# Attention in a diffusion trunk: 128-row low-part score products and a TensorE order written by hand

## The chip, the cores and the metric

One core of one Trainium2 chip runs the whole program in one launch. The metric is device time in microseconds (us); smaller is better. Five engines work side by side, each through its own queue in order: PE (TensorE: matrix products and transposes), DVE (VectorE), ACT (ScalarE), POOL (GpSimd) and SP (which issues the transfers). PEld is the loading of the stationary operand, which runs beside PE.

## The reference

The model has four layers over 256 context tokens and 256 latent tokens of 1024 features, all in float32. The third layer mixes the tokens by grouped-query attention: 16 query heads and 4 key heads of 64 features, so four query heads share a key head. Context queries see the 256 context keys, latent queries see all 512. Queries and keys are normed per head, and those of latent tokens are rotated (`rope`).

```python
def sdpa(q, k, v):
    s = jnp.einsum('bkgqd,bksd->bkgqs', q, k).astype(jnp.float32) * ATTN_SCALE
    p = jax.nn.softmax(s, axis=-1).astype(v.dtype)
    return jnp.einsum('bkgqs,bksd->bkgqd', p, v)
...
        q, k, v = jnp.split(z, [ATTN_Q_DIM, ATTN_Q_DIM + ATTN_KV_DIM], axis=-1)
        q = rms_norm(q.reshape(B, L, ATTN_KV_HEADS, ATTN_GROUP, ATTN_HEAD_DIM), g_q).transpose(0, 2, 3, 1, 4)
        k = rms_norm(k.reshape(B, L, ATTN_KV_HEADS, ATTN_HEAD_DIM), g_k).transpose(0, 2, 1, 3)
...
        if rope:
            q = apply_rope(q, cos, sin)
            k = apply_rope(k, cos, sin)
...
    y_ctx = merge(sdpa(qc, kc, vc))
    k_all = jnp.concatenate([kc, kl], axis=2)
    ob = lax.map(lambda qq: sdpa(qq, k_all, v_all), qb)
```

The other layers (two of gated linear attention, one of convolution), the squared-ReLU MLP behind each, and the modulation are not touched by the change.

## The kernel before

Activations and weights are split exactly into a high part (12 bits, written as float32r) and a low part, and a product is made of three: high with high, low with high, high with low. Tokens stand in four tiles of 128: t=0 and 1 are context, t=2 and 3 latent.

The attention layer (`attn`) projects keys and values first (`prep_kv`), then the queries of eight heads; the other eight heads' queries (`q_steps`) are projected in chunks of six products that `plan` spreads among the first steps of the score loop. `turned` transposes blocks of queries or keys on PE into PSUM, and `evac` copies them out: on ACT, but each EV-th (EV = 100) on DVE.

Queries are kept as 128 rows: 64 rows of the high part and 64 of the low part of the same head (`q2`; in the other order for odd key heads). The keys' high part stands twice, one copy under the other (`k2`), so one product over 128 rows gives high with high and low with high. The keys' low parts of two key heads lie one under the other in one tile (`kl`), and the third product reads the 64 rows of its head alone:

```python
r = slice(64 * (kv % 2), 64 * (kv % 2) + 64)
mm(out=sc[b][:, 0:nk * P], lhsT=q[r], rhs=kl[kv // 2][r, 0:nk * P], start=False, stop=True)
```

The score loop has 32 steps: eight pairs of heads (`hp`), and for each the token tiles in the order t = 2, 3, 0, 1. A step's scores (line 1197 with `k2`, line 1199 with `kl`, for both heads) have 512 columns for latent and 256 for context queries; softmax follows (maximum on DVE, exponential with its sum on ACT, reciprocal and scaling on DVE). `values` then transposes the probabilities (`pTp`, line 1220, 128 x 128 each: eight in a latent step, four in a context step), copies them out (`pT`), and multiplies with the values (`o`, line 1226, of which each fills 64 of the 128 output rows; again eight or four). The loop calls `values` LAG = 3 steps behind the scores:

```python
pend.append((hp, t, o, scores(hp, t)))
if len(pend) > LAG:
    second(*pend.pop(0))
```

This sets priorities only. A scheduler at build time puts each engine's instructions into their final order. In it one `o` product is often followed by transposes, the other `o` products and more transposes, and the scores of one step are split around them. The two heads' `o` products of a chunk stand next to each other in the source, and write the upper and the lower 64 rows of the output.

PSUM has two banks for transposes, four for scores (the fourth from step 12 on), and two that take turns for `o`. `st` tiles come from a pool of 45.

Of the kernel before, what the change touches and what calls it, by code (L numbers as in the profile page):

```python
# [14 lines left out]
P = 128  # L15
# [14 lines left out]
# columns of the packed per-feature parameters  # L30
# [34 lines left out]
LAG = 3  # L65
EV = 100
# [11 lines left out]
def kernel(ctx: ExitStack, tc: tile.TileContext, io, out, depth=8):  # L78
# [19 lines left out]
    def load_table(name):  # L98
        """Loads a table once for the functions traced from here on: behind those traced before."""
        load = nc.scalar.preload_act_table_set(name)  # L100
        for user in table["users"]:
            behind(load.ins, user)
        table.update(name=name, load=load.ins.name, users=[])
# [67 lines left out]
    # work that may run whenever the tensor engine would wait: the next layers' modulation  # L171
# [49 lines left out]
    def project(srcs, acts, streams, done, first=3, extra=0, tail=0, apart=False, then=None):  # L221
        """Feature-major products of the units in srcs with acts. The first few run side by side, so
        that they start with the first activations; apart, the streams of the first few and of the
        last few run one after the other, next to the other stream's norm."""
# [30 lines left out]
    def project_tm(srcs, acts, parts, done, between=lambda z: None, order=(0, 1, 2, 3), before=None):  # L255
        """Token-major products [token, 512] of four units of two k each; parts are lists of token
        tiles that run one after the other."""
# [36 lines left out]
    def mod_sum(i, b, n, kk, got):  # L294
        """The same on VectorE, for the time when the tensor engine is full: both streams' sums over
        the feature tiles, whose partitions the tensor engine adds up at the end."""
# [72 lines left out]
    def spread(cols, blocks, tag="nr"):  # L369
        """[token, block] columns to rows, the same on all partitions."""  # L370
        ps = bank("rows", tag)
        for n, b in enumerate(blocks):
            mm(out=ps[:, b * P:b * P + P], lhsT=cols[:, n:n + 1].to_broadcast([P, P]), rhs=ident,
               start=True, stop=True)
        return ps

    def sums(srcs, blocks):
        """Sums over features (the partitions of all srcs) to [token, block]."""
# [9 lines left out]
    def square(k, zs):  # L388
        """Adds the squares of x's feature tile k, as soon as it is final, to the sums for the norm."""
# [30 lines left out]
    def normed(n, z, rs=None):  # L420
        """The norm of stream z ahead of sub-layer n."""
# [9 lines left out]
    def out_project(n, srcs, acts, streams, gate, bias=None, **kw):  # L431
        """The last product of sub-layer n, added to x, and the next sub-layer's norm."""
# [52 lines left out]
    def gla(i, j, last, first=None):  # L485
# [6 lines left out]
        # low-rank gates, four copies of the rank rows  # L492
# [14 lines left out]
        def start_with(kk):  # L507
            """The norm of two feature tiles as soon as their modulation is there."""
# [7 lines left out]
        # values, token-major  # L516
# [15 lines left out]
        # cumulative log gates  # L532
# [48 lines left out]
        def r_unit(m):  # L581
            def done(ps):
                # the Silu with the functions of the gates' table: r exp(-ln(1 + exp(-r)))
# [11 lines left out]
        def weave(*threads):  # L595
            """Emits threads of steps side by side, the first thread's step first."""
# [5 lines left out]
        def blocks(tl, c, lo=0):  # L602
            """The chunks c of each block from lo on."""
            return tl.rearrange("p (b c t) -> p b c t", c=2, t=CH)[:, lo:, c]

        def prep(hh):
            """Decayed queries and keys and the states of a head, a thread per direction. Tiles of
            which a direction needs only one chunk per block hold both directions."""
            shared = {}

            def direction(d):
# [10 lines left out]
                def products():  # L622
# [11 lines left out]
                    # queries: with the decay since the chunk's start, then since the block's  # L634
# [4 lines left out]
                def ends():  # L639
                    kb, ebv, kd, kx, e = got["kb"], got["ebv"], shared["kd"], b, got["e"]  # L640
                    # keys: with the decay to the chunk's end, then to the block's
# [19 lines left out]
                def carry():  # L661
                    # states ahead of each block, in the direction's order
# [19 lines left out]
        def core(hh):  # L682
            op, at = [], {}

            def inner(bl):
# [12 lines left out]
                # within a chunk: forward up to the query, backward from it on, both at it  # L698
# [71 lines left out]
        # the rank rows in two parts of 12 bits, so that one product with the weights' parts holds  # L770
        # all four products of the parts
# [23 lines left out]
    def conv(i):  # L795
# [29 lines left out]
        def on_dve(c, zs):  # L825
            """The steps of a feature tile's depthwise convolution on VectorE."""
# [21 lines left out]
        def split(c, zs):  # L848
            """Both parts of u of each stream, with zeros around it."""
# [11 lines left out]
        def on_pe(c, zs):  # L861
            """The same on the tensor engine, with diagonal matrices."""
# [26 lines left out]
        # [tile, tap, high or low part], the middle tap first  # L889
# [12 lines left out]
        def merge(old, new):  # L902
            """Puts the steps of new between those of old: the taps of a tile wait for one another."""
# [30 lines left out]
        def layer_norm(z):  # L934
            """The steps of the LayerNorm over features and the Silu."""
# [47 lines left out]
            def staged(*stages):  # L983
                """One step per tile; each stage a tile, or as many as its lag, behind the one before."""
# [12 lines left out]
        def norm_with(z, *queues):  # L997
            """The LayerNorm, with steps of other work between its steps."""
# [21 lines left out]
    def attn(i):  # L1020
# [7 lines left out]
        # [position, q or k, lat tile, feature]: gain times cos, and the signed gain times sin for  # L1028
        # the half-swapped operand
# [345 lines left out]
```

## Time and profile before

| what | value |
|---|---|
| time, median of 3 runs | 2244.36 us (2243.71 to 2244.63) |
| span of the profiled execution | 2243.1 us |
| PE busy | 2194.2 us, 98% |
| DVE busy | 1627.2 us, 73% |
| ACT busy | 871.5 us, 39% |
| PE in the chain that ended last | 90% of the span |
| granted PE clock, mean | 0.990 |

The profiled execution is shown by its span, from its first to its last instruction; the median of the timed runs is 1.3 us above it, which is what lies around the instructions. A PE record begins when the product begins and its end is modelled, so neighbouring products overlap in the records: the price of a product is read from the start of one to the start of the next.

### The profile page before, as it was taken

To read this page: it belongs to the slowest core of one execution; us is meant where nothing else is said; L and a number is where in the kernel's file an instruction comes from. 1 tells how busy PE (TensorE), PEld (TensorE's weight loads), DVE (VectorE), ACT (ScalarE), POOL (GpSimd) and SP (SyncE) were. 2 spreads that over 40 slices of the span, in tenths; PEclk is the share of its full clock that TensorE was granted. 3 is DMA by queue.
4 is the path that set the end of the run, shared out by engine and by line. 5 is a ranking of instruction groups with operands and counts; after the bars stand their busy time and mean duration, and the time that the engine had idled before them with its cause. 6 is when DMAs were issued, how large, how long until landed. Compare 5 with 4: busy or idle time off the path is not lost.

```text
span 2243.1 us, 33453 instructions
## 1 busy us (share of the span) xinstructions
PE 2194.2 (98%) x13154; PEld 1858.6 (83%) x13154; DVE 1627.2 (73%) x2968; ACT 871.5 (39%) x1504; POOL 56.6 (3%) x68
## 2 busy tenths in 40 slices
PE   6999999999999979999999999999999999999999
PEld 5777898888888979988888876688888889899999
DVE  4565577788869986768888677647788776687665
ACT  4443343223232205532232367634232324555443
POOL 0000000000000251000000000000000000000000
PEclk9999999999999979999999999999999999999999
DMA  8543334555522111345555211014465552233553
GB/s 302 170 150 132 116 101 153 177 178 195 198 95 82 33 38 39 105 156 171 179 189 195 85 50 54 20 48 150 142 196 182 194 169 77 93 113 127 186 182 119
DMA packets 83966, 299.58 MB, mean 134 GB/s; under 512 B 9440, under 2 KB 10976, under 8 KB 83808
## 3 DMA queue, kind: packets, MB, share of 16 engines
q1 hardware_dynamic: 83808, 297.44, 40.0%
q8 instruction: 104, 1.70, 0.3%
q14 instruction: 54, 0.44, 0.1%
HBM read 296.35 MB, written 1.05 MB: 133 GB/s over the span
## 4 chain that ended last, share of the span: by engine, by line
PE 90%; DVE 7%; ACT 1%; issue 1%; POOL 0%; DMA 0%; SPq 0%; DVEq 0%; POOLq 0%
PE ps L217 21%; PE ps L218 21%; PE ps L219 21%; DVE cv L841 4%; PE one L217 2%; PE one L218 2%; PE one L219 2%; PE ps L274 2%; PE ps L276 2%; PE ps L275 2%; PE o L1226 2%; PE pTp L1220 1%; PE cvps L881 1%; PE o L718 1%; PE modps L291 1%; PE sc L1199 1%
## 5 line engine op out<-in xcount | busy, mean ns | idle before, releaser
L109 ACT ACTIVATE whi<-raw 128x1024 fp32r<-128x1024 f32 x366 | 387.1, 1059 | 887.3 <-PE ps L218 621.5
L196 DVE TENSOR_TENSOR wlo<-raw,whi 128x1024 fp32r<-128x1024 f32 x366 | 445.1, 1225 | 164.3 <-ACT whi L109 163.3
L217 PE MATMUL ps<-hi,whi 128*128 128x512 f32 (+1 forms) x1336 | 464.1, 348 | 0.0
L219 PE MATMUL ps<-hi,wlo 128*128 128x512 f32 (+1 forms) x1336 | 461.5, 346 | 0.0
L218 PE MATMUL ps<-lo,whi 128*128 128x512 f32 (+1 forms) x1336 | 461.3, 345 | 0.0
L217 PE MATMUL ps<-hhi,whi 128*128 128x512 f32 (+1 forms) x1240 | 437.8, 355 | 3.3 <-ACT hhi L109 3.3
L218 PE MATMUL ps<-hlo,whi 128*128 128x512 f32 (+1 forms) x1240 | 438.4, 354 | 0.0
L219 PE MATMUL ps<-hhi,wlo 128*128 128x512 f32 (+1 forms) x1240 | 436.8, 353 | 0.0
L307 DVE SCALAR_TENSOR_TENSOR macc<-modraw,cs,macc 128x512 f32<-128x512 f32 x504 | 346.8, 744 | 0.0
L217 PEld LDWEIGHTS ps<-hi,whi 128*128 128x128 f32 x1336 | 252.9, 189 | 33.9 <-issue 3.7
L219 PEld LDWEIGHTS ps<-hi,wlo 128*128 128x128 f32 x1336 | 253.1, 189 | 30.7 <-issue 0.2
L218 PEld LDWEIGHTS ps<-lo,whi 128*128 128x128 f32 x1336 | 253.2, 190 | 29.8
L217 PEld LDWEIGHTS ps<-hhi,whi 128*128 128x128 f32 x1240 | 234.4, 190 | 38.4 <-ACT hhi L109 4.0
L219 PEld LDWEIGHTS ps<-hhi,wlo 128*128 128x128 f32 x1240 | 235.2, 190 | 31.6
L218 PEld LDWEIGHTS ps<-hlo,whi 128*128 128x128 f32 x1240 | 235.5, 190 | 30.9
L448 DVE SCALAR_TENSOR_TENSOR x<-ps,mod,x 128x256 f32<-128x256 f32 x264 | 118.6, 480 | 173.6 <-PE ps L219 172.1
L841 DVE SCALAR_TENSOR_TENSOR cv<-u,par,cv 128x498 f32<-128x498 f32 (+28 forms) x210 | 129.4, 679 | 0.4
L109 ACT ACTIVATE hi<-sq 128x512 fp32r<-128x512 f32 (+1 forms) x128 | 73.8, 576 | 104.4 <-DVE sq L463 104.4
L217 PE MATMUL one<-hhi,whi 128*128 128x512 f32 (+1 forms) x256 | 95.2, 372 | 0.3 <-DVE r L588 0.3
L203 DVE TENSOR_TENSOR lo<-sq,hi 128x512 fp32r<-128x512 f32 (+1 forms) x128 | 79.3, 620 | 22.1 <-ACT hi L109 22.1
L218 PE MATMUL one<-hlo,whi 128*128 128x512 f32 (+1 forms) x256 | 91.6, 358 | 0.0
L219 PE MATMUL one<-hhi,wlo 128*128 128x512 f32 (+1 forms) x256 | 91.1, 356 | 0.0
(213 smaller groups left out, 2792.4 us busy)
## 6 DMA issues: line engine op xcount, KB each, us to landing
modraw<-in_w_mod SPq DMA_DIRECT2D x192, 512.0 KB, 3.7
raw<-in_w_mlp_in SPq DMA_DIRECT2D x128, 512.0 KB, 4.1
raw<-in_w_mlp_out SPq DMA_DIRECT2D x128, 512.0 KB, 3.5
raw<-in_conv_pw SPq DMA_DIRECT2D x24, 512.0 KB, 3.4
raw<-in_gla_v SPq DMA_DIRECT2D x16, 512.0 KB, 3.7
raw<-in_gla_r SPq DMA_DIRECT2D x16, 512.0 KB, 3.8
raw<-in_gla_out SPq DMA_DIRECT2D x16, 512.0 KB, 3.9
raw<-in_attn_qkv SPq DMA_DIRECT2D x12, 512.0 KB, 3.4
```

The costliest lines, as they stand in the source:

```text
L109: ins = nc.scalar.activation(**kw).ins
L196: tt(out=lo, in0=raw, in1=hi.bitcast(F32), op=ALU.subtract)
L203: tt(out=lo[:, cols], in0=src, in1=hi.bitcast(F32)[:, cols], op=ALU.subtract)
L217: mm(out=o, lhsT=wh[:, wsl], rhs=ah[:, cols], start=first, stop=False)
L218: mm(out=o, lhsT=wh[:, wsl], rhs=al[:, cols], start=False, stop=False)
L219: mm(out=o, lhsT=wl[:, wsl], rhs=ah[:, cols], start=False, stop=last)
L274: mm(out=ps[t], lhsT=ah[:, tok], rhs=wh[:, sl], start=kk == order[0] and i == 0, stop=False)
L275: mm(out=ps[t], lhsT=al[:, tok], rhs=wh[:, sl], start=False, stop=False)
L276: mm(out=ps[t], lhsT=ah[:, tok], rhs=wl[:, sl], start=False, stop=kk == order[-1] and i == 1)
L307: stt(out=acc, in0=raw[:, h], scalar=c, in1=acc, op0=ALU.mult, op1=ALU.add)
L448: stt(out=x[:, m, c], in0=src[:, c], scalar=gate[:, m, z:z + 1], in1=x[:, m, c], op0=ALU.mult, op1=ALU.add)
L841: ins = stt(out=a3[:, :, lo:hi], in0=u3[:, :, lo + s:hi + s], scalar=tap, in1=a3[:, :, lo:hi], op0=ALU.mult, op1=ALU.add).ins
```

## The change

There are two parts. First, the low parts of the keys are doubled as the high parts already are: `klo` holds each head's 64 features twice (one more ACT copy in each of four token tiles), `turned` makes four transposes of it instead of two, there are four `kl` tiles instead of two, and the low-part product contracts all 128 rows. It then also adds low with low.

Second, `values` is cut into `turned_p` (transposes and copies) and `values` (products). The score loop is put in a `manual_schedule` for PE, so that PE's order is the source's: in step n the scores of n, the value products of n-3, the transposes of n-2 (LAG_T = 2, LAG_O = 1). The other engines are still ordered by the scheduler. Besides, EV goes from 100 to 5, so that each fifth copy out of PSUM is made by DVE.

```diff
-LAG = 3
-EV = 100
+LAG_T = 2
+LAG_O = 1
+EV = 5
...
-        q2, k2, kl = {}, [st("k2", FR) for _ in range(4)], [st("kl", FR) for _ in range(2)]
+        q2, k2, kl = {}, [st("k2", FR) for _ in range(4)], [st("kl", FR) for _ in range(4)]
...
-                tt(out=lo.rearrange("p (h e) -> p h e", e=64), in0=got["q"], in1=h4.bitcast(F32)[:, :, 0],
-                   op=ALU.subtract)
+                tt(out=l4[:, :, 0], in0=got["q"], in1=h4.bitcast(F32)[:, :, 0], op=ALU.subtract)
+                act(out=l4[:, :, 1], in_=l4.bitcast(F32)[:, :, 0], func=ACTF.Copy)
...
-                r = slice(64 * (kv % 2), 64 * (kv % 2) + 64)
-                mm(out=sc[b][:, 0:nk * P], lhsT=q[r], rhs=kl[kv // 2][r, 0:nk * P], start=False, stop=True)
+                mm(out=sc[b][:, 0:nk * P], lhsT=q, rhs=kl[kv][:, 0:nk * P], start=False, stop=True)
...
+        def turn_scores():
+            hp, t, o, ps = scored.pop(0)
+            turned_.append((hp, t, o, turned_p(ps, t)))
+
+        def add_values():
+            hp, t, o, pts = turned_.pop(0)
+            values(pts, hp, t, o)
...
-                pend.append((hp, t, o, scores(hp, t)))
-                if len(pend) > LAG:
-                    second(*pend.pop(0))
+        with tc.manual_schedule(engines={mybir.EngineType.PE}):
...
+                    scored.append((hp, t, o, scores(hp, t)))
+                    if len(turned_) >= LAG_O:
+                        add_values()
+                    if len(scored) > LAG_T:
+                        turn_scores()
```

Three places show the order before and after. On PE, two steps (t = 2 and 3) of the seventh pair of heads, where no query projection is left; `sc<-k` and `sc<-kl` are the two score products, `o<-pT` a value product, `pTp` a transpose. Before:

```order
L1197 MATMUL sc<-k_11190,q_12074 128x512
L1199 MATMUL sc<-kl,q_12074 128x512
L1197 MATMUL sc<-k_11190,q_12074 128x512
L1226 MATMUL o<-pT,vt 64x128 x4
L1220 MATMUL pTp<-ident,p 128x128 x8
L1199 MATMUL sc<-kl,q_12074 128x512
L1197 MATMUL sc<-k_11190,q_12249 128x512
L1199 MATMUL sc<-kl,q_12249 128x512
L1197 MATMUL sc<-k_11190,q_12249 128x512
L1199 MATMUL sc<-kl,q_12249 128x512
L1226 MATMUL o<-pT,vt 64x128
L1220 MATMUL pTp<-ident,p 128x128 x3
```

With the change, the same two steps:

```order
L1198 MATMUL sc<-k_11190,q_12108 128x512
L1199 MATMUL sc<-kl,q_12108 128x512
L1198 MATMUL sc<-k_11190,q_12108 128x512
L1199 MATMUL sc<-kl,q_12108 128x512
L1230 MATMUL o<-pT,vt 64x128 x8
L1219 MATMUL pTp<-ident,p 128x128 x4
L1198 MATMUL sc<-k_11190,q_12287 128x512
L1199 MATMUL sc<-kl,q_12287 128x512
L1198 MATMUL sc<-k_11190,q_12287 128x512
L1199 MATMUL sc<-kl,q_12287 128x512
L1230 MATMUL o<-pT,vt 64x128 x4
L1219 MATMUL pTp<-ident,p 128x128 x4
```

Each step's scores now stand together, and then its value products and its transposes, each in one run.

On DVE, a stretch of the steady part (`mx` a maximum, `den` a reciprocal, the `TENSOR_SCALAR` a scaling). Before:

```order
L1204 TENSOR_REDUCE mx<-sc 128x1 x2
L1208 RECIPROCAL den<-den 128x1
L1209 TENSOR_SCALAR p<-p,den 128x512
L1208 RECIPROCAL den<-den 128x1
L1204 TENSOR_REDUCE mx<-sc 128x1
L1209 TENSOR_SCALAR p<-p,den 128x512
L1204 TENSOR_REDUCE mx<-sc 128x1
L1208 RECIPROCAL den<-den 128x1 x2
L1209 TENSOR_SCALAR p<-p,den 128x256 x2
```

With the change:

```order
L1204 TENSOR_REDUCE mx<-sc 128x1 x2
L1208 RECIPROCAL den<-den 128x1
L1209 TENSOR_SCALAR p<-p,den 128x512
L1208 RECIPROCAL den<-den 128x1
L1209 TENSOR_SCALAR p<-p,den 128x512
L1204 TENSOR_REDUCE mx<-sc 128x1 x3
L1208 RECIPROCAL den<-den 128x1
L1178 COPY pT<-pTp 128x256
L1209 TENSOR_SCALAR p<-p,den 128x512
```

The two scalings of a latent step now stand ahead of the next step's maxima, and a copy of transposed probabilities has come in among them.

On PE at the loop's first steps, `qT` being the transposes of queries that the next scores read. Before:

```order
L1096 MATMUL qT<-ident_r,q2t 128x128 x8
L1162 MATMUL q_11826<-whi,hhi 128x512
L1163 MATMUL q_11826<-whi,hlo 128x512
L1164 MATMUL q_11826<-wlo,hhi 128x512
L1162 MATMUL q_11826<-whi,hhi 128x512
L1163 MATMUL q_11826<-whi,hlo 128x512
L1164 MATMUL q_11826<-wlo,hhi 128x512
L1162 MATMUL q_11826<-whi,hhi 128x512
L1197 MATMUL sc<-k_11187,q_11838 128x512
```

With the change:

```order
L1164 MATMUL q_11850<-whi,hlo 128x512
L1165 MATMUL q_11850<-wlo,hhi 128x512
L1097 MATMUL qT<-ident_r,q2t 128x128 x8
L1198 MATMUL sc<-k_11187,q_11862 128x512
L1199 MATMUL sc<-kl,q_11862 128x512
```

The seven projection products that stood between the transposes and the scores now stand ahead of the transposes or behind the scores.

## Rows read from the trace of the kernel before

**Rows 1.** The page's head and its first part: busy time, share of the span and instructions of an engine.

```profile
span 2243.1 us, 33453 instructions
PE 2194.2 (98%) x13154; PEld 1858.6 (83%) x13154; DVE 1627.2 (73%) x2968; ACT 871.5 (39%) x1504; POOL 56.6 (3%) x68
```

**Rows 2.** The busy time of each engine in three stretches of the score loop: its first four pairs of heads, one steady pair (hp = 6), and the last pair with the rest. Columns: stretch, its length, busy time (number of instructions) of PE, PEld, DVE, ACT, POOL, then granted clock, DMA share and GB/s.

```profile
1340.10:1403.00 62.90, 60.49 (x373) 39.93 (x372) 46.84 (x134) 44.34 (x122) 0.00 (x0) 1.00 0.16 53
...
1429.80:1443.10 13.30, 13.30 (x90) 8.50 (x89) 8.26 (x25) 8.47 (x25) 0.00 (x0) 1.00 0.00 1
1443.10:1468.80 25.70, 25.69 (x184) 16.96 (x183) 10.49 (x31) 13.75 (x39) 0.00 (x0) 1.00 0.00 1
```

**Rows 3.** The instructions of lines 1197 and 1226 on PE: count, duration in ns (least, median, most), first and last start in us, forms (stationary operand, then moving operand). A value product leaves two records, a score product one.

```profile
L1197 PE MATMUL sc<-k,q x64: 276/388/506, 1340.1 to 1454.3; 128*128 128x512 f32 x32, 128*128 128x256 f32 x32
...
L1226 PE MATMUL o<-pT,vt x384: 272/273/325, 1358.5 to 1468.8; 128*64 128x128 f32 x192
```

**Rows 4.** PE in order of time through two steps of a steady pair (hp = 6), and further on in the same pair. Columns: start, duration, engine, line, operation, names, forms, records merged in one row. `128*128`, `64*128` and `128*64` are the shapes of the stationary operand.

```profile
1429.83 0.48 PE L1197 MATMUL sc<-k,q 128*128 128x512 f32 x1
1430.24 0.49 PE L1199 MATMUL sc<-kl,q 64*128 64x512 f32 x1
1430.66 0.51 PE L1197 MATMUL sc<-k,q 128*128 128x512 f32 x1
1431.09 0.66 PE L1226 MATMUL o<-pT,vt 128*64 128x128 f32 x8
1431.68 1.09 PE L1220 MATMUL pTp<-ident,p 128*128 128x128 f32 x8
1432.71 0.49 PE L1199 MATMUL sc<-kl,q 64*128 64x512 f32 x1
1433.13 0.50 PE L1197 MATMUL sc<-k,q 128*128 128x512 f32 x1
1433.56 0.50 PE L1199 MATMUL sc<-kl,q 64*128 64x512 f32 x1
1433.99 0.50 PE L1197 MATMUL sc<-k,q 128*128 128x512 f32 x1
1434.42 0.49 PE L1199 MATMUL sc<-kl,q 64*128 64x512 f32 x1
1434.84 0.43 PE L1226 MATMUL o<-pT,vt 128*64 128x128 f32 x2
1435.21 0.55 PE L1220 MATMUL pTp<-ident,p 128*128 128x128 f32 x3
1435.68 1.09 PE L1226 MATMUL o<-pT,vt 128*64 128x128 f32 x14
1436.70 0.77 PE L1220 MATMUL pTp<-ident,p 128*128 128x128 f32 x5
1437.22 0.36 PE L1197 MATMUL sc<-k,q 128*128 128x256 f32 x1
...
1442.25 0.65 PE L1226 MATMUL o<-pT,vt 128*64 128x128 f32 x6
1442.83 0.55 PE L1220 MATMUL pTp<-ident,p 128*128 128x128 f32 x3
1443.13 0.48 PE L1197 MATMUL sc<-k,q 128*128 128x512 f32 x1
```

**Rows 5.** PE in order of time where the stationary operand keeps its shape: query projection of 512 columns, then the transposes of keys and the product behind them, then the last MLP with 256 columns. Columns as in rows 4.

```profile
1322.07 0.39 PE L274 MATMUL ps<-whi,hhi 128*128 128x512 f32 x1
1322.30 0.39 PE L275 MATMUL ps<-whi,hlo 128*128 128x512 f32 x1
...
1325.48 0.46 PE L1096 MATMUL kT<-ident_r,khi 128*128 128x128 f32 x4
1325.78 0.34 PE L1096 MATMUL kT<-ident_r,klo 128*128 128x128 f32 x2
1325.95 0.47 PE L1162 MATMUL q<-whi,hhi 128*128 128x512 f32 x1
...
2149.83 0.28 PE L218 MATMUL ps<-lo,whi 128*128 128x256 f32 x1
2149.95 0.28 PE L219 MATMUL ps<-hi,wlo 128*128 128x256 f32 x1
```

**Rows 6.** Groups of DVE instructions from 1403 us to 1470 us, shapes apart. Columns: line, engine, operation, names, shapes, count, busy us, mean ns of one, idle time of the engine before them and what ended it.

```profile
L1204 DVE TENSOR_REDUCE mx<-sc 128x1 f32<-128x512 f32 x16 | 10.9, 682 | 4.1 <-PE sc L1199 4.0
L1209 DVE TENSOR_SCALAR p<-p,den 128x512 f32<-128x512 f32 x16 | 7.4, 481 | 0.1
...
L1177 DVE COPY pT<-pTp 128x512 f32<-128x512 f32 x1 | 0.7, 691 | 2.7 <-PE pTp L1220 2.7
```

**Rows 7.** The same view of ACT in the same stretch.

```profile
L109 ACT ACTIVATE p<-sc,mx 128x512 f32<-128x512 f32 x16 | 11.0, 705 | 0.0
L109 ACT ACTIVATE pT<-pTp 128x512 f32<-128x512 f32 x19 | 10.4, 602 | 7.7 <-PE pTp L1220 7.7
...
L109 ACT ACTIVATE pT<-pTp 128x256 f32<-128x256 f32 x22 | 8.0, 387 | 11.8 <-PE pTp L1220 11.8
```

More of the change, by code (lines that the diff above doesn't have):

```diff
@@ L1104, in parts @@
                 nc.vector.tensor_copy(out=vt[t], in_=got["src"][:, 256:512])
-                hi, lo = st("khi", FR), ap_.tile([P, 256], FR, tag="state", name="klo", bufs=12)
-                h4 = hi.rearrange("p (h z e) -> p h z e", z=2, e=64)
+                hi, lo = st("khi", FR), st("klo", FR)
+                h4, l4 = [v_.rearrange("p (h z e) -> p h z e", z=2, e=64) for v_ in (hi, lo)]
                 for z in range(2):
                     act(out=h4[:, :, z], in_=got["q"], func=ACTF.Copy)
-                tt(out=lo.rearrange("p (h e) -> p h e", e=64), in0=got["q"], in1=h4.bitcast(F32)[:, :, 0],
-                   op=ALU.subtract)
+                tt(out=l4[:, :, 0], in0=got["q"], in1=h4.bitcast(F32)[:, :, 0], op=ALU.subtract)
+                act(out=l4[:, :, 1], in_=l4.bitcast(F32)[:, :, 0], func=ACTF.Copy)
                 def turn_k():
                     for src_, dst in ((hi, k2), (lo, kl)):
-                        tp = turned(src_, "kT", len(dst))
+                        tp = turned(src_, "kT")
                         for c, d in enumerate(dst):
@@ L1211, in scores, with turned_p @@
             return ps
-        def values(ps, hp, t, o):
+        def turned_p(ps, t):
             nk = 2 if t < 2 else 4
-            kv = hp // 2
             pts = []
@@ L1223, in values @@
                 pts.append(pT)
+            return pts
+        def values(pts, hp, t, o):
+            nk = 2 if t < 2 else 4
+            kv = hp // 2
             for c in range(nk):
@@ L1227, in values @@
                        rhs=pts[b][:, c * P:c * P + P], start=c == 0, stop=c == nk - 1)
-        pend = []
-        def second(hp, t, o, ps):
-            values(ps, hp, t, o)
-            if t == 1:
+        scored, turned_ = [], []
+        def turn_scores():
[4 more added lines that the diff above has]
+            values(pts, hp, t, o)
+            if t == ORDER_T[-1]:
                 y.append(split(o, st))
@@ L1246, in attn @@
             f()
-        for hp in range(8):
-            o = bank("o", ("nr", "md")[hp % 2])
-            for n, t in enumerate(ORDER_T):
-                for f in plan[4 * hp + n]:
-                    f()
-                pend.append((hp, t, o, scores(hp, t)))
-                if len(pend) > LAG:
-                    second(*pend.pop(0))
-        while pend:
-            second(*pend.pop(0))
+        with tc.manual_schedule(engines={mybir.EngineType.PE}):
+            for hp in range(8):
+                o = bank("o", ("nr", "md")[hp % 2])
+                for n, t in enumerate(ORDER_T):
+                    for f in plan[4 * hp + n]:
+                        f()
+                    scored.append((hp, t, o, scores(hp, t)))
[3 more added lines that the diff above has]
+                        turn_scores()
+            while scored or turned_:
+                if turned_:
+                    add_values()
+                if scored:
+                    turn_scores()
         out_project(2 * i, [io["attn_out"][m] for m in range(8)], y, (0, 1), modt[i][:, 16:24])
```

## The prediction

> **What bounds the kernel now.** The page's head comes first: PE is busy for 2194.2 of 2243.1 us, DVE for 73% of it [rows 1]. A kernel whose PE is never idle gets faster only if PE's own work becomes cheaper, and a busy record does not say whether it is cheap. So the second view is the score loop in stretches [rows 2]: in a steady pair of heads PE is busy for all of 13.30 us, DVE for 8.26, ACT for 8.47. The third is PE in order of time, read from start to start [rows 4], against places where nothing changes [rows 5].
>
> Where the stationary operand keeps its shape, a 512-column product starts 0.23 us after the one before it (0.227 over a long run) and a 256-column one 0.12 us [rows 5]. In the score loop a 512-column product is followed after 0.41 to 0.43 us, whether the 128-row one is followed by the 64-row one or the other way round [rows 4]. The same products, the same columns, the same clock (granted 1.00, [rows 2]): the difference of 0.2 us comes at each change of shape. The loop has three shapes: 128x128 (first score product, transposes, projections), 64x128 (low-part score product) and 128x64 (value product).
>
> **The price of a change of shape.** Value products: three take 0.58 us from their start to the transposes' start (1442.25 to 1442.83), seven take 1.02 (1435.68 to 1436.70), with the same neighbours, so one costs 0.44/4 = 0.11 us. Transposes: eight from 1431.68 take 1.03 us to a change, three from 1442.83 take 0.30 without one; I take 0.11. From 1429.83 to 1437.22 are 7.39 us, with 8 score products of 512 columns (1.82), 12 value products and 16 transposes (28 x 0.11 = 3.08). The other 2.49 us belong to the 13 changes of shape that the rows show, 0.192 us each [rows 4].
>
> The loop as a whole, from the first score product at 1340.1 to the last value product at 1468.8, takes 128.7 us [rows 3]. In the order of the kernel before there stand between these two 64 score products of 512 columns and 64 of 256, 43 projections, 56 query transposes, 192 transposes, 192 value products and 14 products of the next layer step: 14.5 + 7.7 + 9.8 + 4.8 + 42.2 + 3.2 = 82.2 us (a transpose of float32r at 0.085, as the two that take 0.17 [rows 5]). There are 217 changes of shape: 41.7 us. Together 123.9; the 4.8 us left over are waits, of which the first stretch shows 2.4 as idle [rows 2].
>
> **Part 1, low parts doubled.** All 128 places where the 64-row product is entered or left in the old order concern the shape 64x128. With that shape gone, 111 of the 217 changes would remain, since some of them turn into a change between the other two. That is 106 x 0.192 = 20.4 us, all on PE, which nothing covers. The columns, and so the streaming time, stay. Added are eight transposes (8 x 0.085 = 0.7 us on PE, in the projection, where PE is full), eight copies and four duplicates on ACT; the last two I take at nothing, because the projection of queries runs on PE meanwhile; without that cover they would cost some 5 us (12 of at most 0.4, the price of a 256-column copy [rows 7]).
>
> The row shows a 64-row product at 0.42 to 0.43 us in this neighbourhood, not below a 128-row one [rows 4]. The Trainium skill's page "TensorEngine Tiling (Array Packing)", section "Theoretical Speedup", speaks against widening: a dimension of at most 64 gives up to 2x when several such products share the array. By that rule 64 products would go from half price to full, 32 x 0.113 + 32 x 0.06 = 5.5 us lost, an estimate; by the rows nothing is lost, because both heads of a step read the same 64 rows one after the other. The same page, "Key Properties", says that changing the tiling mode drains the engine; it gives no price.
>
> **Part 2, the order by hand.** The orders in the section on the change show four runs per step, scores, value products, transposes, scores: two changes of shape a step (from transposes to scores is none). Counted over the whole loop, 65 remain, 46 fewer than with the first part alone: 8.8 us. What PE then has to do: 82.2 + 0.9 (five more projections and one fewer product of the next step lie between the ends) + 65 x 0.192 = 95.6 us. Five projections move from ahead of the first score to behind it, so the comparable figure is 94.7, and PE that never waits would gain 128.7 - 94.7 = 34.0 us.
>
> It will wait, since the other engines come close. In a steady pair PE now has 2.8 (scores) + 5.3 (48 x 0.11) + 8 x 0.192 = 9.6 us. DVE has 8.26 [rows 2] plus a fifth of eight copies, 1.6 at about 0.55 (0.69 for 512 columns [rows 6]) = 9.1. DVE and ACT stand in a fixed order, and PE no longer has other work ready. I walk one pair, with time 0 at the scores of t=2. The maxima take 0.68 each and run to 2.1; the exponentials (0.70) run to 2.8, the second scaling to 3.6. By the new DVE order only then come the maxima of t=3, to 5.0, its exponentials to 5.7; behind these on ACT wait the two copies of the context step transposed meanwhile (0.39 each [rows 7]), to 6.5, a little less where neighbouring records overlap. PE has done 2.61 + 2.17 us of steps and the scores of t=0, and wants those copies at 5.45: a wait of 0.7 to 1.0. In the next step the value products follow copies of 0.60 each and wait 0.3. The other two steps have slack. With a DVE copy that falls among the scalings I take 1.2 us a pair: 10.8 instead of 13.30.
>
> The first four pairs hold the norm and rotation of the second half of the queries on DVE: 46.8 us busy of 62.9 [rows 2]. To it come, counted in the new order, nine copies, one weight split, one split of `o` and four scalings that fall into this stretch now, 7 us, so 54 us of DVE against 45.2 + 26 x 0.192 = 50.2 of PE. At the first steps the scores now stand directly behind the transposes that feed them: three times about 0.65 us of copy (0.60, [rows 7]) that projections covered before. I take 58 us. In these four pairs DVE is the bound, not PE. The last stretch: 16.5 us of PE and 1.8 of waits for the last softmaxes.
>
> **The sum.** Waits: 58 - 50.2 = 7.8, three steady pairs at 1.2 = 3.6, the end 1.8: 13.2 us. Gain 34.0 - 13.2 - 0.7 = 20.1 us. What follows (output projection, MLP, the last layer) keeps its order and is full of PE work, so it starts 20 us earlier and ends 20 us earlier; the profiled span becomes 2223 us. The median lies 1.3 us above the span: 2244.4 - 20.1 = 2224 us. With waits from 6 to 20 us the forecast's own range is 2217 to 2231.
>
> **The rivals.** First, PE never waits: the softmax has two full steps, and DVE is below PE in a steady pair. Then 34.0 - 0.7 = 33.3 us are gained, 2211 us. Against it stands the walk, and DVE's 54 us in the first half.
>
> Second, the softmax chain sets the pace. If every pair waits as long again as in the walk and more, 11.9 us a pair, and the first half takes 62 and the end 20, the loop takes 62 + 35.7 + 20 - 0.9 = 116.8, the gain is 11.9 - 0.7 = 11.2: 2233 us. For it: DVE is then above 75% busy with an order that puts scalings ahead of maxima. Against it: the old loop, at 13.30, shows no wait of PE at all [rows 2], so the chain fits into that with room.
>
> Third, widening does not pay, because the 0.2 us hangs on the place or on the operand and not on the number of rows. Then only the order's 8.8 us are won, with the old waits: 2244.4 - 8.8 + 0.7 = 2236. By the Trainium skill's speed-up rule ("TensorEngine Tiling (Array Packing)", "Theoretical Speedup") 5.5 us more would be lost: 2242, no change. Against both: value products and transposes, which differ in columns, show the price too, and runs of one shape never do [rows 4, 5].
>
> Fourth, slower: the steps run in lockstep. PE is in order; if value products of a step wait behind copies, these behind exponentials on ACT, these behind maxima on DVE, and the next scores cannot start because their banks are held, nothing overlaps. A step of 512 columns then takes 1.1 (scores) + 1.4 + 0.7 + 0.8 (two copies) + 1.5 (value products, transposes) = 5.5 us, one of 256 columns 4.6 by the same sum, a pair 20 us; with half of the way from 10.8 to there it is 15, and 8 x 1.7 = 14 us lost, 2258. It decides once a pair takes over 13.30. Against it: PE does two steps of other work between a score and its transposes.
>
> **How the numbers follow.** Forecast 62%, no wait 12%, the chain 17%, no gain from widening 4%, lockstep 3%, and 2% for things not named. The range runs from the first rival to beyond the second, 2211 to 2235. A difference of 0.2% (4.5 us) is about what a measurement of this kernel can tell from none: faster 0.94, same 0.03 (the third if waits of the new order come on top, and things not named), slower 0.03.
>
> **What would show it.** The low-part product at 0.23 and 0.12 us from start to start; a steady pair at 10 to 11.5 us instead of 13.30; PE's idle time in the loop no longer nil, ended by ACT's `pT` or by DVE's scalings; DVE above 85% in the first four pairs. I am wrong if a 128-row low-part product still takes 0.4, if a pair stays above 12, or if the layers behind give the time back.

## The result and the profile after

The changed kernel takes 2228.26 us (median of 4 runs, 2226.42 to 2229.87), the kernel before 2244.49 beside it: a ratio of 0.992, 95% interval 0.9898 to 0.9942. It is faster by 16.2 us, where 20 were forecast. Executions of most kernels here, the one before too, fall into two groups some 22 us apart, because a stretch of the untouched convolution layer takes longer in some, so below single runs are compared by what follows that layer.

The head of the page after, against [rows 1]:

```profile
span 2228.0 us, 33427 instructions
...
PE 2171.2 (97%) x13162; PEld 1856.8 (83%) x13162; DVE 1636.3 (73%) x2989; ACT 868.8 (39%) x1495; POOL 58.2 (3%) x68
```

PE is busy for 23.0 us less. The score loop after, in stretches (us, then busy time and instructions of PE, its weight loads, DVE, ACT and POOL, then PE's granted clock, DMA share, GB/s), against [rows 2]: the first four pairs, the fifth, the seventh and the last stretch, and behind these four short ones.

```profile
1341.90:1403.30 61.40, 55.20 (x415) 43.76 (x416) 54.70 (x152) 46.59 (x125) 0.00 (x0) 0.94 0.20 69
1403.30:1414.40 11.10, 10.07 (x90) 7.76 (x89) 9.50 (x27) 7.96 (x24) 0.00 (x0) 1.00 0.01 2
1425.50:1436.30 10.80, 9.87 (x92) 7.64 (x90) 8.90 (x27) 8.42 (x25) 0.00 (x0) 1.00 0.01 2
1436.30:1453.60 17.30, 16.82 (x143) 12.48 (x141) 10.04 (x28) 9.68 (x28) 0.00 (x0) 1.00 0.01 1
1340.00:1342.00 2.00, 0.22 (x2) 0.14 (x2) 1.90 (x5) 1.88 (x5) 0.00 (x0) 1.00 0.00 0
1342.70:1346.00 3.30, 3.30 (x11) 2.51 (x10) 2.83 (x9) 1.50 (x4) 0.00 (x0) 0.50 0.00 0
1380.00:1383.50 3.50, 1.07 (x10) 0.83 (x7) 3.50 (x12) 3.50 (x9) 0.00 (x0) 1.00 0.00 0
1383.70:1387.00 3.30, 2.98 (x15) 2.28 (x14) 3.23 (x10) 3.19 (x8) 0.00 (x0) 0.50 0.59 199
```

A steady pair fell from 13.30 us to 11.10 and 10.80, and PE is no longer busy for all of it. The first four pairs hardly gained: 61.4 against 62.9. The last four rows show what the loop before did not have: PE idle for most of the time, and right behind that 3.3 us at a granted clock of 0.50, the 1.2 GHz level.

PE in order of time after (start, length, engine, line, operation, shape, count; in brackets the idle time ahead of it and what ended it), against [rows 4, 5]:

```profile
1341.87 0.50 PE L1198 MATMUL sc<-k,q 128*128 128x512 f32 x1 [1.78 <-ACT q L110]
...
1343.11 0.63 PE L1163 MATMUL q<-whi,hhi 128*128 128x512 f32 x1
1343.54 0.63 PE L1164 MATMUL q<-whi,hlo 128*128 128x512 f32 x1
...
1403.35 0.49 PE L1198 MATMUL sc<-k,q 128*128 128x512 f32 x1
1403.67 0.39 PE L1199 MATMUL sc<-kl,q 128*128 128x512 f32 x1
1403.90 0.39 PE L1198 MATMUL sc<-k,q 128*128 128x512 f32 x1
1404.13 0.40 PE L1199 MATMUL sc<-kl,q 128*128 128x512 f32 x1
1404.46 1.09 PE L1230 MATMUL o<-pT,vt 128*64 128x128 f32 x16
...
1408.20 0.28 PE L1199 MATMUL sc<-kl,q 128*128 128x256 f32 x1
1408.31 0.28 PE L1198 MATMUL sc<-k,q 128*128 128x256 f32 x1
1408.43 0.28 PE L1199 MATMUL sc<-kl,q 128*128 128x256 f32 x1
1409.45 0.43 PE L1230 MATMUL o<-pT,vt 128*64 128x128 f32 x2 [0.74 <-ACT pT L110]
1410.17 0.65 PE L1230 MATMUL o<-pT,vt 128*64 128x128 f32 x6 [0.29 <-DVE pT L1178]
...
1412.25 1.42 PE L1230 MATMUL o<-pT,vt 128*64 128x128 f32 x16
```

Three things stand here. The low-part product is followed after 0.23 us (1403.67 to 1403.90), where the 64-row one took 0.41 to 0.43 [rows 4]. With 256 columns it is followed after 0.11 us (1408.20 to 1408.31), and in the kernel before after 0.31:

```profile
1437.52 0.38 PE L1199 MATMUL sc<-kl,q 64*128 64x256 f32 x1
1437.83 0.39 PE L1197 MATMUL sc<-k,q 128*128 128x256 f32 x1
```

The value products of t=0 wait 0.74 us for ACT's copy and 0.29 for DVE's. At the half clock projections stand 0.43 us apart (1343.11 to 1343.54), though nothing changes shape there.

What PE's weight loads waited for from 1290 us to the end of the loop, with us in total, times, and the longest:

```profile
PEld o L1230 <- ACT pT L110: 11.3, 18, 2.6
...
PEld sc L1198 <- ACT q L110: 3.2, 3, 2.2
PEld o L1230 <- DVE pT L1178: 2.9, 5, 0.9
PEld qT L1097 <- ACT pT L110: 2.1, 3, 0.9
```

The copies of transposed probabilities on ACT are by far the largest. The longest wait for `q`, 2.2 us, stands ahead of the first scores.

### The profile page after: what moved, and what is told of

Its sections match the earlier page's. It is cut to its first block, busy times and chain, and to the rows that moved or that the text cites. A ratio compares the mean times of both kernels' runs of the same rounds, so it can differ in the third digit from the quotient of the medians.

```text
span 2228.0 us, 33427 instructions
## 1 busy us (share of the span) xinstructions
PE 2171.2 (97%) x13162; PEld 1856.8 (83%) x13162; DVE 1636.3 (73%) x2989; ACT 868.8 (39%) x1495; POOL 58.2 (3%) x68
## 4 chain that ended last, share of the span: by engine, by line
PE 88%; DVE 8%; ACT 1%; issue 1%; POOL 0%; DMA 0%; SPq 0%; POOLq 0%; DVEq 0%; ACTq 0%
PE ps L218 22%; PE ps L219 21%; PE ps L220 21%; DVE cv L842 4%; PE one L218 2%; PE one L219 2%; PE one L220 2%; PE ps L275 2%; PE ps L277 2%; PE ps L276 2%; PE o L719 1%; DVE wlo L197 1%; PE modps L292 1%; PE cvps L882 1%; PE sums L383 1%; PE sps L667 1%
## 5 line engine op out<-in xcount | busy, mean ns | idle before, releaser
L197 DVE TENSOR_TENSOR wlo<-raw,whi 128x1024 fp32r<-128x1024 f32 x366 | 445.3, 1226 | 162.1 <-ACT whi L110 160.9
```

Source lines behind the costliest of these rows:

```text
L197: tt(out=lo, in0=raw, in1=hi.bitcast(F32), op=ALU.subtract)
```

## The experiments

Two readings of the profiled executions stand beside the ratio in this table. "Behind" is the time from the first transposes of keys to the end of the span: all that the change can touch, without the convolution layer. The loop is given as its first four pairs, the next three, and the last stretch. "Changes" counts the changes of operand shape on PE in the loop.

| kernel | changes | ratio (95%) | behind, us | loop, us | half clock in the loop, us |
|---|---|---|---|---|---|
| before | 217 | | 935.6 | 62.9; 13.5, 13.3, 13.3; 25.7 | none |
| after | 65 | 0.992 (0.9898 to 0.9942) | 919.2 | 61.5; 11.1, 11.1, 10.7; 17.3 | 3.4 + 3.4 |
| e1_widen_only | 117 | 0.993 (0.9886 to 0.9975) | 919.2 | 54.3; 11.2, 11.0, 11.0; 23.2 | none |
| e2_order_64rows | 167 | 1.0036 (0.9988 to 1.0084) | 942.3 | 69.5; 14.2, 14.5, 12.3; 19.5 | 20.5, and 6.8 ahead of it |
| e3_order_64rows_grouped | 103 | 0.9989 (0.9944 to 1.0034) | 928.3 | 63.1; 11.4, 11.9, 11.6; 18.4 | none, and 6.8 ahead of it |
| e4_ev100 | 67 | 0.9924 (0.9882 to 0.9967) | 919.3 | 61.7; 10.7, 10.8, 10.7; 17.2 | 6.8 |
| e5_lag_o2 | 61 | 0.9916 (0.9879 to 0.9952) | 912.8 | 60.4; 9.7, 9.3, 9.4; 15.8 | 3.4 + 3.4 |
| e6_turn_first | 65 | 0.9933 (0.9898 to 0.9969) | 922.3 | 64.3; 11.1, 11.1, 10.8; 17.3 | 3.4 + 10.2 |
| e7_lag_o2_turn_first | 61 | 0.9922 (0.9885 to 0.9959) | 914.2 | 60.7; 9.7, 9.2, 9.4; 15.8 | 3.4 + 3.4 |
| e8_hand_order_second_half | 85 | 0.9929 (0.99 to 0.9958) | 918.2 | 56.0; 15.1, 11.1, 10.8; 17.3 | 3.4 |
| e9_late_splits | 61 | 0.9889 (0.9875 to 0.9904) | 912.0 | 55.3; 9.7, 9.3, 10.9; 16.9 | 3.4 |
| e10_loose_first_lag_o2 | 83 | 0.9888 (0.9871 to 0.9904) | 910.4 | 54.7; 11.7, 9.3, 9.4; 15.8 | none |
| e11_loose_first_late_splits | 79 | 0.9886 (0.9872 to 0.9901) | 910.9 | 52.8; 10.9, 9.3, 10.9; 16.9 | none |
| e12_spare_products | 61 | 0.989 (0.9875 to 0.9905) | 913.0 | 59.4; 9.7, 9.3, 9.4; 15.8 | 3.4 |

e1 to e4 share one chip and its runs of the kernel before, so do e5 to e8, and e9 to e12. The last four ratios are lower than e5's partly because the kernel before took 2269.62 us there, against 2245.68 beside e5: e12, which is e5 with spare products, stands as e5 does in "behind".

The first four pairs do not hold the same work in every kernel. In the loose order more of the value products and transposes of these pairs come later, and some projections come ahead of the loop: e1 has 12 value products, 16 transposes and 3 projections fewer there than after, some 3.8 us by the prices of the prediction (the kernel before 12, 16 and 5, some 4.2 us).

**e1: the first part alone**, on the kernel before, which keeps its loose order, LAG = 3 and EV = 100.

```diff
-        ... [st("kl", FR) for _ in range(2)]
+        ... [st("kl", FR) for _ in range(4)]
...
-                mm(out=sc[b][:, 0:nk * P], lhsT=q[r], rhs=kl[kv // 2][r, 0:nk * P], start=False, stop=True)
+                mm(out=sc[b][:, 0:nk * P], lhsT=q, rhs=kl[kv][:, 0:nk * P], start=False, stop=True)
```

> The kernel before, with the keys' low parts doubled and nothing else (loose order, LAG 3, EV 100). In its order 117 changes of operand shape are left in the score loop of 217. Theory A (each change of shape costs PE 0.19 us, whatever the product): 100 x 0.19 = 19 us less on PE, 0.7 us more for transposes, and some of it lost again to waits for the softmax: 2226 to 2232 us. Rival C (the hand-written order is what helped, and widening does little): 2240 us or more.

Widening alone gives what the whole change gives: 919.2 us behind, as after. The loop takes 110.6 us, after 111.7. Its stretches (columns as above), first four pairs, fifth, last:

```profile
1363.90:1418.20 54.30, 51.82 (x374) 39.03 (x374) 46.83 (x134) 44.05 (x122) 0.00 (x0) 1.00 0.16 51
1418.20:1429.40 11.20, 11.07 (x89) 7.91 (x89) 9.40 (x28) 9.54 (x29) 0.00 (x0) 1.00 0.40 134
1451.40:1474.60 23.20, 23.18 (x180) 15.89 (x179) 10.44 (x31) 13.53 (x39) 0.00 (x0) 1.00 0.00 1
```

PE is busy nearly throughout and the clock stays at 1.00.

**e2: the order by hand alone**, with the low part at 64 rows as before.

```diff
...
-                mm(out=sc[b][:, 0:nk * P], lhsT=q, rhs=kl[kv][:, 0:nk * P], start=False, stop=True)
+                r = slice(64 * (kv % 2), 64 * (kv % 2) + 64)
+                mm(out=sc[b][:, 0:nk * P], lhsT=q[r], rhs=kl[kv // 2][r, 0:nk * P], start=False, stop=True)
```

> The changed kernel with the 64-row low-part product put back (order by hand, EV 5), 167 changes of shape in the loop against 65. Theory A: 102 x 0.19 = 19.6 us more PE work than with the change, part of which fills waits that are there now: a steady pair about 12.3 us, 2238 to 2244 us. Rival B (the 64-row product is dear by itself, 0.2 us each, wherever it stands): 64 x 0.2 = 13 us more, 2234 to 2240. Rival C (the order does it): near 2230.

By itself the order is no gain: the interval holds 1, and "behind" is 6.7 us more than before. Of these 4.5 us stand ahead of the loop, where PE waits 3.00 us for a weight split on DVE and then runs at the half clock (so it does in e3). The loop has 50 changes fewer than before, worth 9.6 us, and yet takes 130.0 us instead of 128.7, 20.5 of them at the half clock. The wait and the half clock ahead of the loop, then the fifth pair, and three of its us:

```profile
1356.55 0.69 PE L1165 MATMUL q<-wlo,hhi 128*128 128x512 f32 x1 [3.00 <-DVE wlo L197]
...
1356.70:1363.50 6.80, 6.11 (x14) 4.33 (x15) 6.10 (x16) 3.35 (x9) 0.00 (x0) 0.50 0.25 81
...
1436.30:1450.50 14.20, 14.20 (x90) 9.61 (x89) 8.87 (x27) 8.30 (x24) 0.00 (x0) 0.80 0.01 2
...
1438.00:1441.00 3.00, 3.00 (x18) 1.90 (x18) 1.80 (x4) 1.56 (x4) 0.00 (x0) 0.50 0.00 0
```

**e3: e2 with its low-part products grouped**: both high-part products of a step, then both low-part ones. The products stay 64 rows deep, but 64 changes of shape go.

```diff
...
             for b in range(2):
...
-                mm(..., lhsT=q, rhs=k2[kv][:, 0:nk * P], start=True, stop=False)
-                mm(..., lhsT=q[r], rhs=kl[kv // 2][r, 0:nk * P], start=False, stop=True)
+                mm(..., lhsT=qs[b], rhs=k2[kv][:, 0:nk * P], start=True, stop=False)
+            for b in range(2):
+                mm(..., lhsT=qs[b][r], rhs=kl[kv // 2][r, 0:nk * P], start=False, stop=True)
```

> As e2_order_64rows, but in each step both 128-row score products come first and both 64-row ones after them: the same products, 103 changes of shape instead of 167. Theory A: 64 x 0.19 = 12 us less PE work than e2, so a steady pair of 11.2 to 11.6 us and 2230 to 2235 us. Rival B (the product itself is dear): the same time as e2 within 2 us.

Against e2 this gives 14.0 us behind and 11.9 by the lowest run of each (2249.26 and 2237.37). That is no clean price for 64 changes, since the loop has no half clock (e2's has 20.5 us), and more waiting in its place: PE is idle for 10.4 us in it instead of 5.1. The clean reading is PE in order of time, in a step at full clock:

```profile
1418.55 0.71 PE L1199 MATMUL sc<-k,q 128*128 128x512 f32 x2
1419.19 0.73 PE L1201 MATMUL sc<-kl,q 64*128 64x512 f32 x2
1419.85 1.45 PE L1232 MATMUL o<-pT,vt 128*64 128x128 f32 x16
```

Two 128-row products take 0.64 us up to the change, and two 64-row ones 0.66: twice 0.227 and one change of 0.19 and 0.21. It is the change that is dear and not the 64-row product; the theory that the product itself costs 0.42 falls.

**e4: no copies on DVE**: `EV = 5` back to `EV = 100`.

> The changed kernel with all copies out of PSUM on ACT again (EV 100). Theory: DVE is the bound in the first four pairs, and losing 7 us of copies there lets it run 2 to 4 us shorter: 2224 to 2226 us. Rival: PE's waits are ended by the copies, which stand behind exponentials on ACT; with a fifth more of them there, each step waits longer: 2230 to 2234 us.

No difference, in the ratio, behind (919.3) or in the first four pairs (61.7 against 61.5). So neither DVE's extra copies nor the share of copies left to ACT sets their length.

**e5: one step more between a transpose and the value products**: `LAG_O = 1` to `LAG_O = 2`.

> The changed kernel with LAG_O = 2: the value products of a step come two steps behind its transposes instead of one, so they no longer follow directly on the copies that they read. Theory D (value products wait for copies made in the step before): the waits of PE ended by pT copies go, a steady pair takes 9.7 to 10.3 us, 2218 to 2223 us. Rival E (the transposes wait for the same copies, since only two banks hold them, so the wait only moves): 2226 to 2230 us.

The loop falls from 111.7 to 104.6 us, and behind to 912.8. First four pairs, fifth and sixth pair, and two short stretches of the first four:

```profile
1341.20:1401.60 60.40, 53.71 (x399) 42.72 (x400) 52.75 (x151) 45.95 (x125) 0.00 (x0) 0.94 0.21 70
1401.60:1411.30 9.70, 9.55 (x90) 7.36 (x89) 8.61 (x26) 7.05 (x22) 0.00 (x0) 1.00 0.00 1
1411.30:1420.60 9.30, 9.30 (x91) 7.44 (x90) 8.82 (x27) 7.68 (x24) 0.00 (x0) 1.00 0.01 2
...
1380.00:1384.00 4.00, 1.50 (x12) 0.97 (x10) 3.92 (x12) 4.00 (x11) 0.00 (x0) 1.00 0.28 89
1392.00:1396.00 4.00, 1.70 (x13) 1.25 (x14) 3.89 (x11) 2.93 (x10) 0.00 (x0) 1.00 0.09 24
```

A steady pair is PE's own work again, 9.30 of 9.30 us. So the 1.4 to 1.8 us that a pair took above it were the wait of value products for copies one step old. The first four pairs keep 60.4: there PE stands idle while DVE is full, and in the first of the two stretches ACT too.

**e6: transposes of queries ahead of the projections of the same step**, so that their copies should be covered again.

```diff
         plan = {n: [] for n in range(-1, 33)}
-        for n, count in Q_STEPS:
-            plan[n] += [later.pop(0) for _ in range(count)]
         for n, f in zip(TURN_AT, range(4)):
             plan[n].append(turn_next)
+        for n, count in Q_STEPS:
+            plan[n] += [later.pop(0) for _ in range(count)]
```

> The changed kernel with the query transposes of a step ahead of its projection chunk instead of behind it, so six products cover the copy that the scores read. Theory F (the uncovered copy costs three waits and, with the first, a stretch at half clock): PE's idle time at the first four score groups falls from 4 us to under 1.5, 2224 to 2226 us. Rival G (DVE's norm and rotation set the pace there): within 1 us of the changed kernel.

Not faster: the first four pairs take 64.3 us, 2.8 more, with a longer stretch of half clock (10.2), and the lowest run, 2226.87 us, stands where that of after does (2226.42). The longest wait, the 1.8 us ahead of the first scores, is still there. The scores' other waits for `q` fall from 1.1 us to 0.2, but the transposes of queries now wait 2.8 us for the copies of probabilities instead of 1.1: the wait has moved. **e7** joins e5 and e6:

> Both edits of e5 and e6. Theories D and F add up: 2214 to 2220 us. If only one of them holds, that one's time.

It stands as e5 does (median 2223.88 against 2223.60), and 3.7 us below e6 by the lowest runs (2223.16 and 2226.87). Covering the later copies of `q` does not shorten the first half; the lag pays in both orders.

**e8: the first four pairs in the loose order**, the rest by hand.

```diff
-        with tc.manual_schedule(engines={mybir.EngineType.PE}):
-            for hp in range(8):
...
+        pairs(range(4))
+        with tc.manual_schedule(engines={mybir.EngineType.PE}):
+            pairs(range(4, 8))
```

> The changed kernel with PE's order left to the scheduler in the first four pairs of heads and by hand in the last four. If the hand order loses in the first four pairs, where PE still has projections to fill its waits and weight splits for later layers run on ACT and DVE, these take 54 to 56 us as with widening alone, not 61.5: 2219 to 2223 us. If it loses in the steady part as much: 2226 to 2230 us.

The first four pairs fall to 56.0 us with 20 changes of shape more, but the fifth takes 15.1 instead of 11.1. Of 5.5 us 4.0 are given back at the seam. That fifth pair:

```profile
1419.30:1434.40 15.10, 12.93 (x116) 9.64 (x113) 12.48 (x36) 10.52 (x33) 0.00 (x0) 1.00 0.21 71
```

PE has 24 records more in it than in after's seventh (x92): eight value products (two records each) and eight transposes that the loose part left over, 1.8 us at 0.11 each. It also stands idle for 2.17 us instead of 0.93, 1.23 of them in one wait for a copy on DVE.

**e9: e5 with the splits of the next weights placed later.** The first four units of the output projection's weights were split on ACT and DVE in the third pair; here their splits are ordered behind the softmax of the sixth.

```diff
...
+        if late:
+            behind(a_, late["act"], "late splits")
+            behind(d_, late["dve"], "late splits")
...
+        late.update(got_late)
         out_project(2 * i, [io["attn_out"][m] for m in range(8)], y, (0, 1), modt[i][:, 16:24])
+        late.clear()
```

> e5 (LAG_O = 2) with the splits of the first output-projection weights on ACT and DVE put behind the softmax of the sixth pair of heads; before, the four of them stand at the tenth to twelfth step. Theory H (these splits of 1.1 and 1.2 us hold up copies and scalings and starve PE in the third and fourth pair): the first four pairs take 54 to 57 us instead of 60.4, the half-clock stretch at their end goes, 2217 to 2220 us. Rival I (norm and rotation of the queries fill DVE anyway): the gain is under 1.5 us.

The first four pairs fall from 60.4 to 55.3 us: these splits were a load on both engines on which PE waited. The seventh pair and the end give back 2.6 us (10.9 and 16.9 against 9.4 and 15.8), and behind is 912.0 against 912.8. Another 1.7 us stands behind the loop, where a stretch of half clock near the end of the kernel lasts 6.8 us in e9's execution and 3.4 in e5's. The load is mostly moved, not removed.

**e10: e8 with LAG_O = 2.**

> e5 (LAG_O = 2) with PE's order left to the scheduler in the first four pairs. If the hand order is what starves PE there, these take 56 us as in e8_hand_order_second_half, and the steady pairs 9.3 to 9.7: 2217 to 2221 us. If the splits are what starves it, 59 us or more and 2222 to 2225.

First four pairs, fifth, sixth and last stretch:

```profile
1365.00:1419.70 54.70, 52.91 (x389) 40.03 (x387) 48.62 (x142) 43.28 (x119) 0.00 (x0) 1.00 0.18 59
1419.70:1431.40 11.70, 10.66 (x98) 8.30 (x97) 11.07 (x33) 9.01 (x28) 0.00 (x0) 1.00 0.27 90
1431.40:1440.70 9.30, 9.30 (x91) 7.44 (x89) 8.89 (x27) 7.68 (x23) 0.00 (x0) 1.00 0.01 2
1450.10:1465.90 15.80, 15.33 (x152) 11.96 (x150) 11.13 (x33) 10.66 (x31) 0.00 (x0) 1.00 0.01 2
```

This loop takes 100.9 us, all at a clock of 1.00, and behind 910.4, the least of all. The fifth pair holds eight transposes more than a steady pair, left over as in e8. **e11** joins e9 and e10:

> Both edits of e9 and e10. If theory H and the hand order both count: 2214 to 2218 us. If only one does, that one's time.

It is the same as e10 (behind 910.9, loop 100.9).

**e12: e5 with spare work in the idle stretch ahead of the first scores**: eight products of 512 columns whose result is not used, seven of them directly ahead of the scores.

```diff
+        def spare():
+            junk = bank("junk", "md")
+            for c in range(8):
+                mm(out=junk, lhsT=k2[0][:, 0:P], rhs=k2[0], start=c == 0, stop=c == 7)
+
+        plan[0].append(spare)
```

> e5 (LAG_O = 2) with eight products of 512 columns whose result is not used, in the place where PE waits 1.8 us for the first queries' copies; seven of them stand directly ahead of the first scores. Theory J (the idle stretch is what brings the half clock just behind it): the granted clock stays at 1.00 there, and the run is 1 to 2 us faster than e5, though PE does more, 2221 to 2223 us. Rival K (the clock falls anyway, or the products only add): the stretch stays, and 2224 to 2226 us.

PE waits 0.20 us ahead of the first scores instead of 1.78 in after. Its stretches (columns as above) ahead of and behind those scores, and at two later idle places:

```profile
1361.00:1364.00 3.00, 2.80 (x13) 2.00 (x12) 2.33 (x7) 2.24 (x7) 0.00 (x0) 1.00 0.00 0
...
1400.00:1402.00 2.00, 0.66 (x4) 0.42 (x4) 2.00 (x8) 2.00 (x5) 0.00 (x0) 1.00 0.00 0
1402.00:1404.00 2.00, 0.94 (x8) 0.74 (x8) 1.91 (x7) 2.00 (x8) 0.00 (x0) 1.00 0.67 215
1404.00:1406.00 2.00, 2.00 (x21) 1.60 (x20) 2.00 (x5) 2.00 (x5) 0.00 (x0) 1.00 0.85 277
...
1412.00:1414.00 2.00, 0.71 (x4) 0.40 (x4) 2.00 (x6) 2.00 (x7) 0.00 (x0) 1.00 0.03 8
1414.00:1416.00 2.00, 1.16 (x9) 1.02 (x9) 1.72 (x5) 0.76 (x2) 0.00 (x0) 0.87 0.24 43
1416.00:1418.00 2.00, 2.00 (x13) 1.50 (x12) 1.07 (x4) 1.45 (x4) 0.00 (x0) 0.50 0.55 219
```

The half clock behind the first scores is gone. One later idle place (1400 to 1404) was not followed by a lower clock, another (1412 to 1416) was. The first four pairs gain 1.0 us on e5, and behind is 913.0: no gain. Behind the loop it takes 1.1 us more than e5, with the same 6.8 us of half clock near the end as e9.

## Why the prediction came out as it did, step by step

**What bounds the kernel** held. PE was the bound; its busy time fell by 23.0 us, and the time by 16.2.

**The price of a change of shape** held: forecast 0.192 us, in e3's rows 0.19 and 0.21. With it the third rival fell. The speed-up that the Trainium skill's "TensorEngine Tiling (Array Packing)", section "Theoretical Speedup", gives to a dimension of at most 64 shows in no row here: two 64-row products side by side take 0.66 us in e3, two 128-row ones 0.64.

**Part 1** brought all of the gain, though less than it was said to be worth: 20.4 less 0.7 us forecast, 16.4 in e1 by "behind". There the loop takes 18.2 us less than before. That is 100 changes fewer at 0.182 us; I had counted 106 fewer in the old order. The copies and duplicates that were taken at nothing were covered in the loose order: in e8 and e10 33.3 us pass from the first transposes of keys to the first scores instead of 32.6, the price of eight transposes, and PE's longest wait there is 0.69 us in both and before. In after the same stretch takes 33.1, where 0.4 less than before was forecast. What it has too much is the wait of 1.78 us for the copies of `q` ahead of the first scores, sized at 0.65.

**Part 2** gained nothing beside the widening. The work saved is there (52 changes fewer than e1, 10.0 us at 0.192), but PE is idle for 2.6 us in e1's loop and 9.7 in after's, which also has 6.8 us of half clock: 111.7 us against 110.6. Without the widening (e2) it gained nothing either. I gave it 8.8 us and charged the waits to the whole. Its own terms, taken together, are 8.8 us of changes and 4.8 of old waits against 13.2 of new ones: 0.4 us. So the sum already held it to be worth next to nothing, and the text did not say so. Of the new waits:

- Three steady pairs were well sized: 32.9 us instead of 32.4. The wait of 0.74 us at t=0 is where the walk has 0.7 to 1.0; the 0.29 behind it is DVE's copy, charged without a place. e5 shows their cause, the lag of one step, by removing them.
- The end: 17.3 instead of 18.3.
- The first four pairs: 61.5 instead of 58, the largest miss. It is not PE's idle time, which is 6.2 us (61.40 less 55.20) where 7.8 were charged. PE's busy time is 55.2 instead of 50.2, and the half clock can account for at most 3.4 of these 5.0 us; the rest stays open. The reason given was half of one, too. DVE's 54.7 us of work came as forecast, but "In these four pairs DVE is the bound" did not hold: e4 takes 4 us off DVE there and changes nothing. Where PE stands still (1380.0 to 1383.5) DVE and ACT are both full, with splits of the output projection's weights and the norm of queries, and PE's fixed order has nothing to put in. The copy that PE wants stands behind two such splits on ACT:

```profile
1380.26 2.02 ACT L110 ACTIVATE whi<-raw 128x1024 fp32r<-128x1024 f32 x2
...
1383.27 0.43 PE L1230 MATMUL o<-pT,vt 128*64 128x128 f32 x2 [2.43 <-ACT pT L110]
```

- Moving the splits away (e9) takes 5.1 us off these pairs, with the same products in them and one stretch of half clock instead of two. Letting PE reorder there takes 5.5 (e8 against after) and 5.7 (e10 against e5), of which some 2.9 and 2.0 are work that then stands outside these pairs. The uncovered copies of `q`, which I had charged with 2 us, cost 1.1 in the loop and 1.8 ahead of it.
- The half clock was not in the prediction. Two stretches of some 3.4 us at half speed can cost at most about 3.4 us together. The four timed executions fit that: two have a mean granted clock of 0.989 and take 2226.42 and 2226.81 us, two have 0.987 and 0.988 and take 2229.72 (the profiled one) and 2229.87. Where the clock fell in the other three is not on record. e12 removes one stretch and gains 1.0 us in these pairs, none in all.

The sum: the loop fell short of its forecast by 2.9 us (111.7 instead of 108.8), the stretch ahead of it by 0.9, and all that lies ahead of the first transposes of keys took 1.3 us more in the profiled execution. That makes up, to 0.1 us, the difference between the 20.1 us forecast and the 15.1 between the two spans. That the loop came so near is in part luck: PE's idle time was below the waits of the sum, 9.7 instead of 13.2 us, while no term stood for the half clock (at most 3.4) or for the 3 us of PE's busy time that stay open.

**The rivals.** PE without waits did not come, and e5 and e10 show what it would have needed. The chain that sets the pace did not come as priced (11.9 us a pair), though its 62 us for the first half did. Lockstep did not come.

**Better than both.** e5 changes one constant: median 2223.60 us, ratio 0.9916, and 6.4 us less behind than after. e10 stands 8.8 us below after there, yet the medians of e9 to e12, on one chip, lie within 0.9 us (2243.53 to 2244.41), so the times do not tell these four apart.

**Open.** How much of the first four pairs is the half clock and how much the waits that bring it; and why one idle stretch in e12 was followed by a lower clock and another was not.

## What to carry to other kernels

Read PE from start to start, not by its busy share: where neighbouring products differ in the shape of their stationary operand, each change cost about 0.2 us, and widening an operand with copies of itself removes it. An order fixed by hand for PE needs a lag that spans the copies between its steps (two steps here, not one), and loose order where other engines are full. Count what such an order adds in waits against what a scheduler does with the cheaper operands alone, since here that was already the whole gain.

## What was not expected of the hardware

The granted clock fell to 0.50 inside a loop that had run at 1.00. In after this came right behind places where PE had done 0.22 us of work in 2.00 and 1.07 in 3.50, and lasted about 3.4 us; products of 512 columns then stood 0.43 us apart instead of 0.23. In e2's loop such stretches come to 20.5 us. The loops with the loose order ahead (before, e1, e10, e11) show none, e8 one; e3's, by hand throughout, shows none though PE is idle for 10.4 us in it. Not each idle stretch brings it, as e12 shows too.
